# Strassen on four of eight blocks in the second MLP product, with a new way out of PSUM for its results

## The chip, the core and the metric

The kernel runs on one core of a Trainium2 chip, in one launch. The metric is the device time of a run in microseconds (us). Five engines matter: TensorE (PE in the profile, its weight loads PEld), VectorE (DVE), ScalarE (ACT), and SyncE (SP), which issues the weight transfers. GpSimd (POOL) has next to nothing to do.

## The reference

Two layers over 256 tokens of width 2048, all in float32. Each layer is a mixer and a dense MLP, each behind an RMS norm and added to the residual stream. The mixers (a short convolution beside differential attention in layer 0, forgetting attention in layer 1) are not touched by the change. The MLP is

```
def _sqrelu_mlp(h, w1, w2):
    return jnp.square(jax.nn.relu(h @ w1)) @ w2
...
        h = _rmsnorm(x, norm2_g[l])
        x = x + _sqrelu_mlp(h, mlp_w1[l], mlp_w2[l])
```

with `w1` of 2048 x 8192 and `w2` of 8192 x 2048, in both layers.

## The kernel before

**Precision.** A float32 product is made of three matmuls on split operands: each operand is a high part (a copy rounded to fp32r) and a low part (the rest), and `products` adds high x high, high x low and low x high into one PSUM bank (L635, L636, L637). The weights arrive as float32 in a tile `raw` (1 MB, 3 buffers). `split_w` makes `wh` on ScalarE (L146) and, from it, `wl` on VectorE (L147), 3 buffers each, so a split can start only when TensorE is through with the tile three back.

**The MLP.** `mlp` goes over 4 groups of 2048 hidden units. In a group, `hidden` makes 8 blocks of 256 hidden units by the first product (`gemm_t`, L564 and L568), and each block's result is squared, split and put away (`take`, `fill`). Then `gemm_pair` makes the second product twice: for output columns 0 to 1023 (n = 0) and 1024 to 2047 (n = 2). Here these two are called the first and the second product of a group, and their blocks 0 to 7. There are 16 products in all, 8 in each layer.

**Two kinds of block.** A block is 256 hidden units by 1024 output columns, for 256 tokens. `KINDS` says how each is made. Kind C is plain: 8 products into four banks, 24 matmuls. Kind S is Strassen's method: 7 products, 21 matmuls, into the banks P2, Q3, Q4 (shared with C blocks) and P1, Q5, P7, P6 (for S alone). For it VectorE first makes four sums of weights in a tile `T` (L652, L654, L655), and a second split is made, of `T` (`wb`), beside that of the weights (`wa`). P1, P2 and Q3 use `wa`, the first half of a block; Q5, P7, P6 and Q4 use `wb`, the second half.

```
    KINDS = "SCSCSCCC"
```

**Ends of a product.** When the last S block is done, its four own banks are added up in SBUF (tile `E`, L681 to L684) and added to the residual `xr` (L689): the early sums. The four shared banks are added to `xr` by four VectorE instructions that read PSUM (`final`, L695). `final` is put on the list `late`, which `flush` empties in the next product, behind the splits of its first block.

**Order.** The code is written as one stream, and the tile framework's scheduler then sets the order on each engine. It moves instructions past each other on an engine, single matmuls too, but each engine's queue then runs in that order. The order on VectorE is the same in the two products of all 8 groups.

Of the kernel before, what the change touches and what calls it, by code (L numbers as in the profile page):

```python
# [16 lines left out]
P = 128  # L17
D = 2048
# [8 lines left out]
def trunk_kernel(  # L27
# [54 lines left out]


    pending = []
    late = []

    def flush():

        while late:
            late.pop(0)()  # L90

    def step():

# [56 lines left out]
    def gemm(acts, w, c0, first=False):  # L150

        acc = []
        total = 4 * len(acts)
        i = 0
        for ai, a in enumerate(acts):
            raw = wraw.tile([P, 4, CW], F32, name="raw")
            src = w[a.row:a.row + CW, c0:c0 + CW].rearrange("(k p) n -> p k n", p=P)
            if first and ai == 0:
                for h in range(4):
                    nc.sync.dma_start(raw[:, h, :], src[:, h, :])  # L160
            else:
                nc.sync.dma_start(raw, src)
            wh, wl = split_w(raw, parts=4 if first and ai == 0 else 2 if first else 1)
            if i == 0:
                flush()
                acc += [accp.tile([P, CW], F32, name="acc") for _ in range(2)]
            until(lambda: a.left <= 0)
            if first and ai == 0:
                idle(6)
            for h in range(2):  # L170
                kk = (2 * h, 2 * h + 1)

                seq = [(t, k, p) for k in kk for p in (0, 2, 1) for t in range(2)]
# [65 lines left out]
    nlam = const.tile([P, 1], F32, name="nlam")  # L239
    bfb = const.tile([P, 16], F32, name="bfb")  # L240
    GP = 16 * 32 + 96
    gw = const.tile([P, KT, 16], F32, name="gw")
    gws = const.tile([P, GP], F32R, name="gws")

    def setup():
        rows = work.tile([P, 2 * P], F32, name="y")[:, :P]
        lv = work.tile([P, 12 * P], F32, name="ob", bufs=1)[:, :2 * P].rearrange("p (v d) -> p v d", v=4)
        nc.scalar.dma_start(rows[0:32], norm2_g.rearrange("l (k p) -> (l k) p", p=P))
        nc.scalar.dma_start(rows[32:56], hyb_conv_w[0].rearrange("w (k p) -> (w k) p", p=P))
        for c in range(0, P, 64):  # L250
            nc.scalar.dma_start(rows[56:57, c:c + 64], hyb_dq_g)
            nc.scalar.dma_start(rows[57:58, c:c + 64], hyb_dk_g)
        nc.scalar.dma_start(rows[58:59], hyb_subln_g)
        nc.scalar.dma_start(rows[59:60], fox_q_g)
        nc.scalar.dma_start(rows[60:61], fox_k_g)
        for i, v in enumerate((hyb_lq1, hyb_lk1, hyb_lq2, hyb_lk2)):
            nc.scalar.dma_start(lv[:, i, :], v.broadcast_to([P, 64]))
        nc.scalar.dma_start(bfb, fox_b_f.broadcast_to([P, 16]))
        nc.scalar.dma_start(gw, fox_w_in[0, :, 3 * D:3 * D + 16].rearrange("(k p) n -> p k n", p=P))


        nc.gpsimd.memset(mask, 0.0)
        for b in (0, 2):
            nc.gpsimd.affine_select(
                out=mask[:, b * P:(b + 1) * P], in_=mask[:, b * P:(b + 1) * P], pattern=[[-1, P]],
                compare_op=ALU.is_ge, fill=NEG, base=0, channel_multiplier=1)
        nc.gpsimd.memset(ones, 1.0)
        nc.gpsimd.affine_select(
            out=triu, in_=ones, pattern=[[1, P]], compare_op=ALU.is_ge, fill=0.0, base=0,
            channel_multiplier=-1)  # L270
        yield
# [153 lines left out]

    def forget_gates(nm):

        wv = gws[:, :KT * 32].rearrange("p (k n) -> p k n", n=32)
        nc.scalar.copy(gws[:, KT * 32:], ones[:, :96])
        nc.scalar.copy(wv[:, :, 0:16], gw)  # L430
# [115 lines left out]
    def gemm_t(acts, w, c0):  # L546
# [3 lines left out]
        for c in range(2):  # L550
            raw = wraw.tile([P, 8, 2 * P], F32, name="raw")
            r0 = c * 8 * P
            nc.sync.dma_start(raw, w[r0:r0 + 8 * P, c0:c0 + 2 * P].rearrange("(k p) n -> p k n", p=P))
            wh, wl = split_w(raw, (8, 2 * P))
            if c == 0:
                flush()
                acc += [accp.tile([P, CW], F32, name="acc") for _ in range(2)]
            for h in range(2):
                a = acts[2 * c + h]
                until(lambda: a.left <= 0)  # L560
                for f, k, p in TORDER:
                    fs = slice(f * P, (f + 1) * P)
                    if p == 0:
                        nc.tensor.matmul(  # L564
                            acc[f], wh[:, 4 * h + k, fs], a.both[:, k, :, :].rearrange("p s t -> p (s t)"),
                            start=c + h + k == 0, stop=False)
                    else:
                        nc.tensor.matmul(acc[f][:, 2 * P:], wl[:, 4 * h + k, fs], a.hi[:, k, :], start=False,  # L568
                                         stop=(c, h, k) == (1, 1, 3))
                step()  # L570
# [1 line left out]

    KINDS = "SCSCSCCC"

    class PairS:

# [27 lines left out]
    def hidden(nm, w, c0):  # L606

        pairs, half = [], None
        for i, kind in enumerate(KINDS):
# [2 lines left out]
                p = PairS()  # L612
            elif half is not None:
                p, half = PairC(half), None
            elif "C" in KINDS[i + 1:]:
                t = actp.tile([P, 4, 2, 2 * P], F32R, name="act")
                p, half = PairC(t[:, :2]), t[:, 2:]
            else:
# [17 lines left out]
        nc.tensor.matmul(acc, a[0], b[1], start=False, stop=False)  # L636
        nc.tensor.matmul(acc, a[1], b[0], start=False, stop=last)  # L637

    def gemm_pair(pairs, w, r0, n, r2, done):

        B = {}
        live = set()
        for i, (kind, p) in enumerate(zip(KINDS, pairs)):
# [12 lines left out]
                wa, wb = split_w(raw[:, 1:4]), split_w(T)  # L656
            else:
                wa = split_w(raw)
            if i == 0:
                flush()  # L660
                for nm in ("P2", "Q3", "Q4", "X"):
                    B[nm] = accp.tile([P, CW], F32, name="acc")
                for nm in ("P1", "Q5", "P7", "P6"):
# [11 lines left out]
            else:  # L675
                for k in range(2):
                    for bank, t, h in (("P2", 0, 1), ("Q3", 0, 0), ("X", 1, 0), ("Q4", 1, 1)):
                        mul(bank, p.part(k, t), wa, 2 * k + h, not more and k == 1)
            if i == KINDS.rindex("S") + 1:
                E = qkv.tile([P, 4, CW], F32, name="qk")  # L680
                nc.scalar.copy(E[:, 3], B["P1"])  # L681
                nc.vector.tensor_tensor(E[:, 2], B["P6"], E[:, 3], ALU.add)
                nc.vector.tensor_tensor(E[:, 1], B["P7"], E[:, 2], ALU.add)
                nc.vector.tensor_tensor(  # L684
                    E[:, 0:3:2], B["Q5"].unsqueeze(1).broadcast_to([P, 2, CW]), E[:, 1:3], ALU.subtract)
                for t in (1, 0):
                    x2 = xall[:, n:n + 2, t, :]
                    e = E[:, 2 - 2 * t:4 - 2 * t]
                    nc.vector.scalar_tensor_tensor(x2, e, r2[:, t:t + 1], x2, ALU.mult, ALU.add)  # L689
                done(0)  # L690
            step()

        def final():
            for bank, m, t in (("P2", n + 1, 0), ("Q3", n, 0), ("X", n, 1), ("Q4", n + 1, 1)):
                nc.vector.scalar_tensor_tensor(  # L695
                    xr[m][:, t, :], B[bank], r2[:, t:t + 1], xr[m][:, t, :], ALU.mult, ALU.add)
                done(1, m, t)
        late.append(final)

    def mlp(nm, l, nxt):  # L700
        ov = out[0].rearrange("(t p) d -> p t d", p=P)
        r2 = None
        for g in range(4):
# [5 lines left out]
            for n in (0, 2):  # L709
                def done(stage, m=None, t=None, n=n, g=g):  # L710
# [7 lines left out]
                        pending.extend([nxt.chunk(0), nxt.chunk(1)])  # L718
                    elif n == 2 and (m, t) == (n + 1, 1):
                        pending.extend([nxt.chunk(2), nxt.chunk(3)])  # L720
                gemm_pair(pairs, mlp_w2[l], g * D, n, r2, done)
        if nxt is None:
            flush()

    def load_x(n):
        if n > 0:
# [69 lines left out]
```

## Time and profile before

| | |
|---|---|
| three runs | median 2175.74 us (2175.13 to 2176.91) |
| profiled execution | 2178.49 us |
| its span, first to last instruction | 2176.8 us |
| TensorE busy | 2166.2 us (100%) |
| VectorE busy | 1547.4 us (71%) |
| ScalarE busy | 1052.7 us (48%) |
| granted TensorE clock | 1.0 of full |

The sums of the prediction are made against the profiled execution, 2178.49 us, which is 2.75 us above the median. Busy shares are means over the whole span: the stages differ.

### The profile page before, as it was taken

How to read it: one execution, taken by the hardware profiler on the slowest of the kernel's cores; microseconds unless marked ns; L12 is line 12 of the kernel's file. 1: busy time of each engine (PE TensorE's matmuls, PEld its weight loads, DVE VectorE, ACT ScalarE, POOL GpSimd, SP SyncE). 2: the span in 40 equal slices, each digit the busy share in tenths (PEclk: the TensorE clock that was granted, in tenths of full speed). 3: DMA queues.
4: the chain of work that ended last, by engine and by line, in shares of the span. 5: the costliest groups of instructions: out<-in, count | busy, mean ns of one | idle time of the engine just before them, and what ended most of it. 6: DMA issues, size and time to landing. Idle time of an engine off the chain costs nothing. (4 is left out here: it accounts for less than half of the span.)

```text
span 2176.8 us, 26071 instructions
## 1 busy us (share of the span) xinstructions
PE 2166.2 (100%) x10738; PEld 1818.3 (84%) x10738; DVE 1547.4 (71%) x1574; ACT 1052.7 (48%) x1101; POOL 19.1 (1%) x17
## 2 busy tenths in 40 slices
PE   9999999999999999999999999999999999999999
PEld 7887888888888888888888888888888888888887
DVE  5666655778769768767855565567787697687687
ACT  6455443544444444445554454445444444444453
POOL 0000000000000000000000000000000000000000
PEclk9999999999999999999999999999999999999999
DMA  8544556555665665665645555555566656656654
GB/s 272 180 159 158 187 177 200 178 167 198 220 193 170 220 193 182 211 189 190 210 163 194 187 183 173 185 166 176 168 207 216 193 174 216 190 191 207 186 192 151
DMA packets 245273, 412.08 MB, mean 189 GB/s; under 512 B 9399, under 2 KB 144802, under 8 KB 245154
## 3 DMA queue, kind: packets, MB, share of 16 engines
q1 hardware_dynamic: 237296, 405.84, 57.6%
q10 hardware_dynamic: 7858, 4.58, 0.7%
q8 instruction: 84, 1.38, 0.3%
q14 instruction: 35, 0.29, 0.0%
HBM read 408.28 MB, written 2.11 MB: 189 GB/s over the span
## 5 line engine op out<-in xcount | busy, mean ns | idle before, releaser
L147 DVE TENSOR_TENSOR wl<-raw,wh 128x2048 fp32r<-128x2048 f32 (+3 forms) x390 | 855.7, 2196 | 476.8 <-ACT wh L146 476.3
L146 ACT CAST wh<-raw 128x2048 fp32r<-128x2048 f32 (+3 forms) x390 | 713.6, 1832 | 654.3 <-PE acc L179 232.0
L564 PE MATMUL acc<-act,wh 128*128 128x512 f32 x2048 | 643.8, 396 | 0.0
L179 PE MATMUL acc<-wh,act 128*128 128x512 f32 x2048 | 565.0, 397 | 0.1
L568 PEld LDWEIGHTS acc<-act,wl 128*128 128x128 f32 x2048 | 384.7, 188 | 90.7
L179 PEld LDWEIGHTS acc<-wh,act 128*128 128x128 f32 x2048 | 376.5, 188 | 75.3 <-issue 2.0
L568 PE MATMUL acc<-act,wl 128*128 128x256 f32 x2048 | 402.4, 278 | 0.0
L179 PE MATMUL acc<-wl,act 128*128 128x512 f32 x1024 | 318.8, 391 | 0.3 <-DVE wl L147 0.3
L564 PEld LDWEIGHTS acc<-act,wh 128*128 128x128 f32 x2048 | 312.3, 189 | 0.8
L636 PE MATMUL acc<-wl,act 128*128 128x512 f32 x656 | 256.1, 390 | 2.1 <-DVE wl L147 1.9
L637 PE MATMUL acc<-wh,act 128*128 128x512 f32 x656 | 255.3, 389 | 0.0
L635 PE MATMUL acc<-wh,act 128*128 128x512 f32 x656 | 251.5, 389 | 0.0
L179 PEld LDWEIGHTS acc<-wl,act 128*128 128x128 f32 x1024 | 192.1, 188 | 42.8 <-issue 0.7
L636 PEld LDWEIGHTS acc<-wl,act 128*128 128x128 f32 x656 | 123.1, 188 | 30.7 <-DVE wl L147 5.2
L635 PEld LDWEIGHTS acc<-wh,act 128*128 128x128 f32 x656 | 123.1, 188 | 25.7
L637 PEld LDWEIGHTS acc<-wh,act 128*128 128x128 f32 x656 | 123.2, 188 | 25.3
L146 ACT CAST wh<-qk 128x2048 fp32r<-128x2048 f32 x48 | 91.8, 1913 | 92.9 <-DVE qk L655 68.7
L147 DVE TENSOR_TENSOR wl<-qk,wh 128x2048 fp32r<-128x2048 f32 x48 | 109.9, 2290 | 22.2 <-ACT wh L146 21.6
L626 ACT COPY qk<-acc 128x256 f32<-128x256 f32 x128 | 47.1, 368 | 132.4 <-PE acc L568 132.4
L635 PE MATMUL tp<-wh,act 128*128 128x512 f32 x192 | 74.7, 389 | 0.0
L636 PE MATMUL tp<-wl,act 128*128 128x512 f32 x192 | 74.7, 389 | 0.0
L637 PE MATMUL tp<-wh,act 128*128 128x512 f32 x192 | 74.7, 389 | 0.0
(173 smaller groups left out, 1434.4 us busy)
## 6 DMA issues: line engine op xcount, KB each, us to landing
raw<-in_mlp_w_dram SPq DMA_DIRECT2D x256, 1024.0 KB, 5.5
raw<-in_fox_w_in_dram SPq DMA_DIRECT2D x48, 1024.0 KB, 5.2
raw<-in_hyb_w_in_dram SPq DMA_DIRECT2D x47, 1024.0 KB, 5.2
raw<-in_hyb_w_out_dram SPq DMA_DIRECT2D x16, 1024.0 KB, 5.2
raw<-in_fox_w_out_dram SPq DMA_DIRECT2D x16, 1024.0 KB, 5.1
ob<-fcd ACTq DMA_DIRECT2D x4, 512.0 KB, 4.5
xr<-in_x_dram SPq DMA_DIRECT2D x3, 512.0 KB, 7.4
raw<-in_hyb_w_in_dram SPq DMA_DIRECT2D x4, 256.0 KB, 4.5
```

Of the source, the lines that this page charges most:

```text
L146: nc.scalar.copy(wh[:, s], src[:, s])
L147: nc.vector.tensor_tensor(wl[:, s], src[:, s], wh[:, s].bitcast(F32), ALU.subtract)
L179: nc.tensor.matmul(acc[t], x, (wl if p == 1 else wh)[:, k, :], start=st, stop=sp)
L564: nc.tensor.matmul(acc[f], wh[:, 4 * h + k, fs], a.both[:, k, :, :].rearrange("p s t -> p (s t)"), start=c + h + k == 0, stop=False)
L568: nc.tensor.matmul(acc[f][:, 2 * P:], wl[:, 4 * h + k, fs], a.hi[:, k, :], start=False, stop=(c, h, k) == (1, 1, 3))
L626: nc.scalar.copy(fj, acc[j][:, 2 * P:])
L635: nc.tensor.matmul(acc, a[0], b[0], start=not started, stop=False)
L636: nc.tensor.matmul(acc, a[0], b[1], start=False, stop=False)
L637: nc.tensor.matmul(acc, a[1], b[0], start=False, stop=last)
```

## The change

1. `KINDS` becomes `SCSSCSCC`: four S blocks and four C blocks, in places 0, 2, 3, 5 and 1, 4, 6, 7.
2. The early sums are made at the head of block 7 (two after the last S block, before the block's matmuls) and no longer behind those of the block after the last S.
3. The four shared banks are taken out of PSUM by ScalarE (four `activation` copies with the scale `r2`, into a tile `F`), and VectorE adds `F` to `xr` in one instruction over 128 x 2048. That addition is put on a second list, `later`, emptied behind the splits of block 1 of what follows. Only the last product of the program ends as before (`tail`).
4. In `hidden`, C blocks 6 and 7 keep their operands in the two `v` buffers. The forget gate's weights are loaded and split in tiles of the pools `work` and `act`, no longer in tiles of their own.

```
-    late = []
-
-    def flush():
-
-        while late:
-            late.pop(0)()
+    late, later = [], []
+
+    def flush(held):
+
+        while held:
+            held.pop(0)()
...
-            if i == 0:
-                flush()
+            if i > 0:
+                flush(later)
+            else:
+                flush(late)
...
-    KINDS = "SCSCSCCC"
+    KINDS = "SCSSCSCC"
...
-            elif "C" in KINDS[i + 1:]:
+            elif i < 3:
...
-    def gemm_pair(pairs, w, r0, n, r2, done):
+    def gemm_pair(pairs, w, r0, n, r2, done, tail):
...
-            if i == KINDS.rindex("S") + 1:
+            if i == 1:
+                flush(later)
+            if i == KINDS.rindex("S") + 2:
                 E = qkv.tile([P, 4, CW], F32, name="qk")
                 nc.scalar.copy(E[:, 3], B["P1"])
                 nc.vector.tensor_tensor(E[:, 2], B["P6"], E[:, 3], ALU.add)
...
         def final():
-            for bank, m, t in (("P2", n + 1, 0), ("Q3", n, 0), ("X", n, 1), ("Q4", n + 1, 1)):
-                nc.vector.scalar_tensor_tensor(
-                    xr[m][:, t, :], B[bank], r2[:, t:t + 1], xr[m][:, t, :], ALU.mult, ALU.add)
-                done(1, m, t)
...
+            F = qkv.tile([P, 4, CW], F32, name="qk")
+            for bank, j in (("P2", 2), ("Q3", 0), ("X", 1), ("Q4", 3)):
+                nc.scalar.activation(F[:, j], B[bank], AF.Copy, scale=r2[:, j % 2:j % 2 + 1])
+
+            def add():
+                x4 = xall[:, n:n + 2].rearrange("p m t n -> p (m t) n")
+                nc.vector.tensor_tensor(x4, x4, F, ALU.add)
+                for j in range(4):
+                    done(1, n + j // 2, j % 2)
+            later.append(add)
         late.append(final)
```

**First place: VectorE in the middle of a first product (layer 0, group 1).** In the rows of before, `wl_5057` is the low part of block 2's sums, `qk_5113` holds the sums of block 4, and `wl_5084` is the low part of block 3, a C block:

```order
L147 TENSOR_TENSOR wl_5057<-qk_5048,wh_5056 128x2048
L600 TENSOR_TENSOR v_4964<-qk_4979,v_4964 128x2x256
L652 TENSOR_TENSOR qk_5113<-raw_5111 128x1024
L654 TENSOR_TENSOR qk_5113<-qk_5113,raw_5111 128x512
L655 TENSOR_TENSOR qk_5113<-qk_5113,raw_5111 128x512
L147 TENSOR_TENSOR wl_5084<-raw_5081,wh_5083 128x2048
L147 TENSOR_TENSOR wl_5118<-raw_5111,wh_5117 128x1536
```

In the changed kernel block 3 is an S block: `qk_5102` holds its sums, `wl_5107` and `wl_5111` are its two low parts, `qk_5167` are the sums of block 5 and `wl_5138` is the low part of block 4:

```order
L147 TENSOR_TENSOR wl_5076<-qk_5067,wh_5075 128x2048
L606 TENSOR_TENSOR v_4983<-qk_4998,v_4983 128x2x256
L658 TENSOR_TENSOR qk_5102<-raw_5100 128x1024
L660 TENSOR_TENSOR qk_5102<-qk_5102,raw_5100 128x512
L661 TENSOR_TENSOR qk_5102<-qk_5102,raw_5100 128x512
L147 TENSOR_TENSOR wl_5107<-raw_5100,wh_5106 128x1536
L658 TENSOR_TENSOR qk_5167<-raw_5165 128x1024
L147 TENSOR_TENSOR wl_5111<-qk_5102,wh_5110 128x2048
L147 TENSOR_TENSOR wl_5138<-raw_5135,wh_5137 128x2048
```

The sums made here are those of block 3 in place of block 4's, and one more instruction of 1024 and one of 2048 stand between block 3's first low part and block 4's.

**Second place: VectorE at the start of a second product (same group).** Before, `wl_5250` and `wl_5254` are the low parts of block 0, `qk_5322` the sums of block 2, and `wl_5293` is the low part of block 1:

```order
L147 TENSOR_TENSOR wl_5250<-raw_5243,wh_5249 128x1536
L655 TENSOR_TENSOR qk_5245<-qk_5245,raw_5243 128x512
L652 TENSOR_TENSOR qk_5322<-raw_5320 128x1024
L654 TENSOR_TENSOR qk_5322<-qk_5322,raw_5320 128x512
L695 SCALAR_TENSOR_TENSOR xr_87<-acc_4987,r2_3711,xr_87 128x512
L147 TENSOR_TENSOR wl_5254<-qk_5245,wh_5253 128x2048
L695 SCALAR_TENSOR_TENSOR xr_87<-acc_4988,r2_3711,xr_87 128x512
L695 SCALAR_TENSOR_TENSOR xr_87<-acc_4990,r2_3711,xr_87 128x512
L695 SCALAR_TENSOR_TENSOR xr_87<-acc_4989,r2_3711,xr_87 128x512
L147 TENSOR_TENSOR wl_5293<-raw_5290,wh_5292 128x2048
```

In the changed kernel `wl_5274` and `wl_5278` are the low parts of block 0, `qk_5281` is `F`, `wl_5318` is the low part of block 1, `qk_5348` and `qk_5383` are the sums of blocks 2 and 3, and `wl_5357` is the second low part of block 2:

```order
L661 TENSOR_TENSOR qk_5269<-qk_5269,raw_5267 128x512
L147 TENSOR_TENSOR wl_5274<-raw_5267,wh_5273 128x1536
L147 TENSOR_TENSOR wl_5278<-qk_5269,wh_5277 128x2048
L714 TENSOR_TENSOR xr_87<-xr_87,qk_5281 128x2048
L147 TENSOR_TENSOR wl_5318<-raw_5315,wh_5317 128x2048
L658 TENSOR_TENSOR qk_5348<-raw_5346 128x1024
L147 TENSOR_TENSOR wl_5353<-raw_5346,wh_5352 128x1536
L660 TENSOR_TENSOR qk_5348<-qk_5348,raw_5346 128x512
L658 TENSOR_TENSOR qk_5383<-raw_5381 128x1024
L661 TENSOR_TENSOR qk_5348<-qk_5348,raw_5346 128x512
L660 TENSOR_TENSOR qk_5383<-qk_5383,raw_5381 128x512
L661 TENSOR_TENSOR qk_5383<-qk_5383,raw_5381 128x512
```

The wide addition now stands between the low parts of blocks 0 and 1, where three of the four PSUM reads stood, and the sums of two blocks follow ahead of `wl_5357`, which is the next row.

**The same place on ScalarE.** Before, the high parts of blocks 0, 1 and 2 of the second product follow one another (`wh_5249` and `wh_5253`, `wh_5292`, `wh_5326` and `wh_5330`):

```order
L146 CAST wh_5249<-raw_5243 128x1536
L146 CAST wh_5253<-qk_5245 128x2048
L146 CAST wh_5292<-raw_5290 128x2048
L146 CAST wh_5326<-raw_5320 128x1536
L146 CAST wh_5330<-qk_5322 128x2048
```

Now the four copies out of PSUM stand among them:

```order
L146 CAST wh_5273<-raw_5267 128x1536
L710 ACTIVATE qk_5281<-acc_5006,r2_3712 128x512
L146 CAST wh_5277<-qk_5269 128x2048
L710 ACTIVATE qk_5281<-acc_5007,r2_3712 128x512
L710 ACTIVATE qk_5281<-acc_5009,r2_3712 128x512
L710 ACTIVATE qk_5281<-acc_5008,r2_3712 128x512
L146 CAST wh_5317<-raw_5315 128x2048
```

The high part of block 0's sums (`wh_5277`) moved behind the first of the copies, and that of block 1 behind all four.

## Rows read from the trace of the kernel before

**Rows 1.** The page's first part: engine, busy us (share of the span), instructions.
```profile
PE 2166.2 (100%) x10738; PEld 1818.3 (84%) x10738; DVE 1547.4 (71%) x1574; ACT 1052.7 (48%) x1101; POOL 19.1 (1%) x17
```
**Rows 2.** Stretches of group 1, layer 0: hidden blocks, first product, second product.
```profile
core 0: us, PE busy (x) PEld busy (x) DVE busy (x) ACT busy (x) POOL busy (x), PEclk, DMA share, GB/s
567.65:656.82 89.17, 89.17 (x514) 77.81 (x513) 60.40 (x61) 40.02 (x39) 0.00 (x0) 1.00 0.61 189
656.82:698.65 41.83, 41.78 (x186) 34.28 (x185) 37.03 (x31) 20.90 (x14) 0.00 (x0) 1.00 0.58 193
698.65:740.16 41.51, 41.51 (x185) 34.35 (x183) 35.72 (x26) 20.49 (x12) 0.00 (x0) 1.00 0.64 211
```
**Rows 3.** L636's own view: its engine's idle time (us, times), by what ended it.
```profile
  DVE wl L147: 7.1, 11
```
**Rows 4.** Timeline, first product: start us, us, engine, line [idle before <- releaser].
```profile
671.79 0.39 PE L635 MATMUL acc<-wh,act 128*128 128x512 f32 x1
...
672.22 0.19 PEld L636 LDWEIGHTS acc<-wl,act 128*128 128x128 f32 x1 [0.47 <-DVE wl L147]
672.22 0.50 PE L636 MATMUL acc<-wl,act 128*128 128x512 f32 x1
```
**Rows 5.** Timeline of VectorE in the first product, from the second low part of block 2.
```profile
664.05 2.29 DVE L147 TENSOR_TENSOR wl<-qk,wh 128x2048 fp32r<-128x2048 f32 x1 [0.42 <-ACT wh L146]
666.26 0.68 DVE L600 TENSOR_TENSOR v<-qk,v 128x512 fp32r<-128x512 f32 x1
667.28 1.23 DVE L652 TENSOR_TENSOR qk<-raw 128x1024 f32<-128x1024 f32 x1 [0.34 <-DMA raw<-in_mlp_w_dram]
668.54 0.69 DVE L654 TENSOR_TENSOR qk<-qk,raw 128x512 f32<-128x512 f32 x1
669.27 0.69 DVE L655 TENSOR_TENSOR qk<-qk,raw 128x512 f32<-128x512 f32 x1
669.88 3.95 DVE L147 TENSOR_TENSOR wl<-raw,wh 128x2048 fp32r<-128x2048 f32 x2
```
**Rows 6.** Timeline of VectorE, end of the first and start of the second product.
```profile
679.71 2.29 DVE L147 TENSOR_TENSOR wl<-raw,wh 128x2048 fp32r<-128x2048 f32 x1 [3.44 <-ACT wh L146]
681.92 0.69 DVE L682 TENSOR_TENSOR qk<-tp,qk 128x512 f32<-128x512 f32 x1
682.52 2.28 DVE L147 TENSOR_TENSOR wl<-raw,wh 128x2048 fp32r<-128x2048 f32 x1
...
688.66 1.21 DVE L652 TENSOR_TENSOR qk<-raw 128x1024 f32<-128x1024 f32 x1
689.79 2.47 DVE L689 SCALAR_TENSOR_TENSOR xr<-qk,r,xr 128x1024 f32<-128x1024 f32 x2
692.18 0.68 DVE L654 TENSOR_TENSOR qk<-qk,raw 128x512 f32<-128x512 f32 x1
692.78 1.75 DVE L147 TENSOR_TENSOR wl<-raw,wh 128x1536 fp32r<-128x1536 f32 x1
694.45 0.68 DVE L655 TENSOR_TENSOR qk<-qk,raw 128x512 f32<-128x512 f32 x1
...
701.75 2.28 DVE L147 TENSOR_TENSOR wl<-raw,wh 128x2048 fp32r<-128x2048 f32 x1
```
**Rows 7.** Timeline of ScalarE in the same stretch.
```profile
677.76 1.91 ACT L146 CAST wh<-raw 128x2048 fp32r<-128x2048 f32 x1 [3.82 <-PE acc L637]
...
687.97 1.49 ACT L146 CAST wh<-raw 128x1536 fp32r<-128x1536 f32 x1 [3.52 <-PE acc L637]
```
**Rows 8.** Timeline of TensorE at block 1 of the second product.
```profile
703.41 1.07 PE L635 MATMUL acc<-wh,act 128*128 128x512 f32 x4
704.31 0.39 PE L635 MATMUL tp<-wh,act 128*128 128x512 f32 x1
704.54 0.39 PE L636 MATMUL acc<-wl,act 128*128 128x512 f32 x1
```
**Rows 9.** Groups by line: busy us, mean ns of one, idle before.
```profile
L695 DVE SCALAR_TENSOR_TENSOR xr<-acc,r,xr 128x512 f32<-128x512 f32 x64 | 44.3, 743 | 5.5 <-PE acc L637 5.5
L229 ACT ACTIVATE qk<-acc,rstd 128x512 f32<-128x512 f32 x32 | 20.7, 683 | 0.9 <-PE acc L179 0.9
```
**Rows 10.** Timeline where layer 0's MLP ends (1086.4) and layer 1's first projection begins.
```profile
1084.79 0.87 DVE L136 SCALAR_TENSOR_TENSOR act<-tp,g,act 128x256 fp32r<-128x256 f32 x2
...
1086.38 0.60 PE L198 MATMUL tp<-ident,xr 128*128 128x128 f32 x4
...
1088.38 0.83 ACT L135 ACTIVATE act<-tp,g 128x256 fp32r<-128x256 f32 x2
```

More of the change, by code (lines that the diff above doesn't have):

```diff
@@ L241, in trunk_kernel @@
     GP = 16 * 32 + 96
-    gw = const.tile([P, KT, 16], F32, name="gw")
-    gws = const.tile([P, GP], F32R, name="gws")
     def setup():
@@ L258, in setup @@
         nc.scalar.dma_start(bfb, fox_b_f.broadcast_to([P, 16]))
-        nc.scalar.dma_start(gw, fox_w_in[0, :, 3 * D:3 * D + 16].rearrange("(k p) n -> p k n", p=P))
         nc.gpsimd.memset(mask, 0.0)
@@ L426, in forget_gates @@
     def forget_gates(nm):
+        gt = actp.tile([P, 16 * P], F32R, name="act")
+        gws = gt[:, :GP]
+        gw = work.tile([P, 2 * P], F32, name="y").rearrange("p (k n) -> p k n", n=16)
+        nc.scalar.dma_start(gw, fox_w_in[0, :, 3 * D:3 * D + 16].rearrange("(k p) n -> p k n", p=P))
+        yield
         wv = gws[:, :KT * 32].rearrange("p (k n) -> p k n", n=32)
@@ L554, in gemm_t @@
             wh, wl = split_w(raw, (8, 2 * P))
-            if c == 0:
-                flush()
+            if c > 0:
+                flush(later)
+            else:
+                flush(late)
                 acc += [accp.tile([P, CW], F32, name="acc") for _ in range(2)]
@@ L658, in gemm_pair @@
                 wa = split_w(raw)
+            if i == 1:
+                flush(later)
+            if i == KINDS.rindex("S") + 2:
+                E = qkv.tile([P, 4, CW], F32, name="qk")
+                nc.scalar.copy(E[:, 3], B["P1"])
+                nc.vector.tensor_tensor(E[:, 2], B["P6"], E[:, 3], ALU.add)
+                nc.vector.tensor_tensor(E[:, 1], B["P7"], E[:, 2], ALU.add)
+                nc.vector.tensor_tensor(
+                    E[:, 0:3:2], B["Q5"].unsqueeze(1).broadcast_to([P, 2, CW]), E[:, 1:3], ALU.subtract)
+                for t in (1, 0):
+                    x2 = xall[:, n:n + 2, t, :]
+                    e = E[:, 2 - 2 * t:4 - 2 * t]
+                    nc.vector.scalar_tensor_tensor(x2, e, r2[:, t:t + 1], x2, ALU.mult, ALU.add)
+                done(0)
             if i == 0:
-                flush()
+                flush(late)
                 for nm in ("P2", "Q3", "Q4", "X"):
@@ L678, in gemm_pair @@
                         mul(bank, p.part(k, t), wa, 2 * k + h, not more and k == 1)
-            if i == KINDS.rindex("S") + 1:
[L680 to L690, printed above, removed]
             step()
         def final():
-            for bank, m, t in (("P2", n + 1, 0), ("Q3", n, 0), ("X", n, 1), ("Q4", n + 1, 1)):
-                nc.vector.scalar_tensor_tensor(
-                    xr[m][:, t, :], B[bank], r2[:, t:t + 1], xr[m][:, t, :], ALU.mult, ALU.add)
-                done(1, m, t)
+            if tail:
+                for bank, m, t in (("P2", n + 1, 0), ("Q3", n, 0), ("X", n, 1), ("Q4", n + 1, 1)):
+                    nc.vector.scalar_tensor_tensor(
+                        xr[m][:, t, :], B[bank], r2[:, t:t + 1], xr[m][:, t, :], ALU.mult, ALU.add)
+                    done(1, m, t)
+                return
+            F = qkv.tile([P, 4, CW], F32, name="qk")
[7 more added lines that the diff above has]
+            later.append(add)
         late.append(final)
@@ L720, in done @@
                         pending.extend([nxt.chunk(2), nxt.chunk(3)])
-                gemm_pair(pairs, mlp_w2[l], g * D, n, r2, done)
+                gemm_pair(pairs, mlp_w2[l], g * D, n, r2, done, nxt is None and g == 3 and n == 2)
         if nxt is None:
-            flush()
+            flush(late)
     def load_x(n):
```

## The prediction

> **What bounds the kernel now.** I read the page's busy times first: TensorE is busy for the whole span, VectorE for 71%, ScalarE for 48% [rows 1]. Then the stretches of one group: in the hidden blocks VectorE has room (60.4 of 89.2 us), but in the two products it is busy for 37.0 of 41.8 and 35.7 of 41.5 us [rows 2]. That is where the change adds VectorE work, so those two lines matter and not the 71%. The second product's stretch holds its 183 matmuls (the row counts two of its neighbours), 41.51 / 183 = 0.2268 us each; I write m for it. An S block is 21 m = 4.76 us, a C block 24 m = 5.44 us. Last, who makes TensorE wait there: the second of the three matmuls of a sum (L636) for the low part of the weights, 11 times, 7.1 us of idle engine in all [rows 3]. In the instance shown the weight load was idle for 0.47 us, but the matmul came 0.43 us after the one before it, so TensorE lost 0.43 - 0.23 = 0.20 us [rows 4]. By that ratio the 7.1 us cost 3.0 us. So TensorE is the bound, and VectorE stands close behind it in the products.
>
> **What is removed from TensorE.** A product has 4 x 21 + 4 x 24 = 180 matmuls, three fewer. 16 products, 48 matmuls, 48 m = **-10.9 us**.
>
> **What VectorE gets.** One more S block in a product: sums of 1.21 + 0.69 + 0.69, a second low part of 2.29, and a first one of 1.75 in place of 2.29, together +4.35 us [rows 5, 6]. The first product then needs 37.0 + 4.35 = 41.4 us of VectorE against 180 m = 40.8 us of TensorE. In the second product the four PSUM reads go (4 x 0.743 us, [rows 9]) and the wide addition comes. Before has no such instruction; the nearest is L147, also two float32 operands in SBUF over 128 x 2048, 2.29 us, and I take that. The upper end is two L689 of 1024, 2.47 us; the lower end is 2.2, L147's distance to the next start. The second product needs 35.7 + 4.35 - 2.97 + 2.29 = 39.4 us. Both together: 80.8 us of VectorE in 81.6 of TensorE. With only three weight tiles ahead, an in-order queue can't be 99% busy without being late, so I follow it through one group. All eight have this order.
>
> The change rests on the copies to SBUF sparing VectorE, and the trace prices that at 2.97 - 2.29 = 0.68 us a product. The Trainium skill (VectorE: DVE Perf Modes, The perf-mode tier table) speaks against more: a float32 addition of two tensors makes one result a cycle, from SBUF as from PSUM, and for 2048 elements it gives 2293 ns. By that figure the sum below stays as it is; if its doubled rate for one source applied (1227 ns), each group would wait 1.07 us less, 8.5 us in all.
>
> **First product.** Clock zero is its first matmul (656.82 before). The VectorE rows up to the hidden result of block 7 (L600) are the same as before; it started at 666.26, so at 9.44. Distances between starts, from the rows: 0.61 after a 512 when the next is independent, 0.73 when it is not; 1.13 and 1.26 after a 1024; 1.67 after 1536; 2.21 after 2048 [rows 5, 6]. Block 3's sums start at 10.05 and their last at 12.04; its first low part at 12.65, block 5's first sum at 14.32, block 3's second low part from 15.45 to 17.74. TensorE wants that after 66 + 9 matmuls and two high-part matmuls that the order has pulled ahead: 77 m = 17.46. **It waits 0.3 us.** The waits of before go: there the sums of block 4 stood in this place and waited for their transfer [rows 5], which made block 3's low part late; block 3's tile was asked for a whole block earlier. So -3.0 us for the old waits, all told.
>
> **Second product.** Clock zero now is the first matmul of block 5 of the first product; the second product begins 69 m = 15.65 later. Block 6's high part may start when block 4 is done; before, block 4 began at 656.82 + 90 m + 0.3 = 677.5, the high part of block 5 waited for that and started 0.2 later, took 1.91, and the low part followed at 679.71 [rows 6, 7]. So block 6's low part starts at 2.15. Nine rows from there without a wait (2.21, 0.60, 2.21, 0.60, 1.13, 1.13, 0.60 and 2.39 for the two that were L689, [rows 6]) bring VectorE to the last sum of block 0 at 13.0, ready at 13.7, and to its first low part, done at 15.4. Its second low part needs ScalarE's high part, and ahead of that stands the copy of P2. That bank's last matmul is over at 15.65 - 10 m + 0.39 = 13.8; the copy costs 0.68 (L229, also from PSUM with a scale, [rows 9]; the next starts 0.62 later), so the high part runs from 14.4 to 16.3. The low part runs to 18.65, the wide addition starts at 18.55, and block 1's low part runs from 20.75 to 23.05. TensorE does 13 matmuls to 18.6, waits 0.15, is in block 1 at 20.6, does four high-part matmuls and one of block 2 ahead (as it did before, [rows 8]), and **from 21.7 waits 1.45 us** for block 1's low part.
>
> It then has 20 + 8 matmuls, to 29.5. VectorE meanwhile: a sum, a low part of 1536, five sums of blocks 2 and 3, to 29.4; block 2's sums were ready at 28.2, so their high part is there at 30.1 and the low part at 32.4. TensorE does four high-part matmuls from 30.15, three of block 3 and sits at 32.5: **1.5 us lost**. 26 matmuls later, at 38.4, block 4 does five, to 39.55, and its low part (queue: 1.67 + 2.21 + 1.13 + 2.29 from 32.3) is there at 39.7: **0.15**. From there VectorE keeps ahead. Lost in a second product: 0.15 + 1.45 + 1.5 + 0.15 = 3.25 us; in a group 3.55; in eight, **+28.4 us**.
>
> **The other edits.** At the end of layer 0's MLP the transposes for the next norm stood among the last blocks' matmuls and their splits ahead of `final`. With later sums they all follow the last matmul, and the first low part (L136, 0.48) stands behind the wide addition, which waits for the four copies: 0.85 + 2.21 + 0.48 = 3.55 after the last matmul. Eight transposes (0.9) and the first high part (0.47 behind the copies, at 1.3) leave TensorE idle for 0.4 and, after two matmuls, from 1.75 for 1.85: **+2.3 us**, once [rows 10]. At nothing: the extra `fill` of an S block in `hidden` (1.5 us of VectorE a group), hidden in the 29 us that VectorE has free there; without that room it would be 12 us. Also at nothing: the gate weights, asked for a whole MLP before use, and the tiles of blocks 6 and 7, whose buffers were last read a group before.
>
> **The sum.** -10.9 - 3.0 + 28.4 + 2.3 = +16.8; 2178.5 + 16.8 = 2195.3 profiled, and 2.75 less for the median: **2192.5 us**, slower by 0.8%. Its own range: the order of the rows is fixed, but each clock above may be off by half a us, and waits may run from 2.3 to 4.8 us a group; the dearer wide addition (+0.2, 1.6 us in all) lies within that. 2183 to 2203.
>
> **The rivals.** (a) *TensorE stays fed; faster.* For it: the busiest engine at 100%, and VectorE would come to about 75% of the span. Then -10.9 and -3.0 come in, the end of layer 0 costs 2.3, and the time is 2164. It needs VectorE ahead at block 1 of the second product, 1.5 us earlier than I find it; the break-even is 11.6 / 8 = 1.45 us lost a group. Against it: 80.8 of 81.6. The Trainium skill (Perfetto Trace Analysis, Identifying the Most-Contended Engine) names this rule, to judge by the engine of highest occupancy; the trace agrees over the span and not in the products. 17%.
> (b) *VectorE loses more:* ScalarE's copies make the high parts of blocks 1 and 2 late as well, and the first product enters late, because block 5's sums are split up between low parts. A further 1.5 us a group gives 2204 or more. For it: ScalarE's order puts block 1's high part behind four copies. Against: it is done at 20.1, before VectorE asks. 13%.
> (c) *The waits are half of mine,* 1.3 to 2.3 us a group: between nothing and +0.3%, 2174 to 2183; the half below 2180 is within 0.2%. 14%.
> (d) *My forecast,* 56%.
>
> **Chances and range.** A difference under 0.2% (4.4 us) is about what a measurement of this kernel can't tell from no change. Faster: 0.17 from (a). Same: 0.08, half of (c) and the upper edge of (a). Slower: the rest, 0.75. The range of 8 in 10 runs from 2172, within (c) and above (a), to 2207.
>
> **What would show it.** In the new profile: 10690 matmuls; TensorE's waits for L147's low part some 29 us in total, most on the second products, block 1 and block 2, none over 2 us; VectorE near 97% busy in the products' stretches; the wide addition at 2.3 us; a gap of about 2 us after layer 0's last product. If the stretches of a second product take 41 us and not 44, the queue walk is wrong, and the likeliest place is block 0's second high part on ScalarE.

## The result, and the profile after

The changed kernel takes 2197.24 us (median of 4 runs, 2195.94 to 2197.40) against 2176.28 us before on the same chip (2175.13 to 2176.91): by all runs compared 1.0093 times as long, 95% interval 1.0080 to 1.0105 (the two medians alone give 1.0096). It is slower. The profiled execution took 2195.94 us with a span of 2194.1 us at full granted clock, 17.3 us more than the span of before.

The page's first part, and the group of the second matmul of a sum for the shared banks (busy us, mean ns | idle before it, and what ended it):

```profile
PE 2169.3 (99%) x10690; PEld 1804.2 (82%) x10690; DVE 1612.1 (73%) x1617; ACT 1112.8 (51%) x1177; POOL 15.4 (1%) x17
...
L642 PE MATMUL acc<-wl,act 128*128 128x512 f32 x448 | 176.5, 394 | 9.3 <-DVE wl L147 9.3
```

48 matmuls are gone, and the page still shows TensorE busy for 3 us more. Part of each wait reads as busy: rows of matmuls are 0.39 us long but start 0.23 apart, so the first 0.16 us of a wait are covered, and a matmul that has waited reads longer (0.50 us below) than one that hasn't. So the time lost is read from the starts of the matmuls. The stretches of group 1 in layer 0 (hidden blocks, first product, second product; columns as in [rows 2]) show where the time went:

```profile
568.21:657.37 89.16, 89.16 (x513) 77.80 (x512) 63.02 (x63) 41.23 (x41) 0.00 (x0) 1.00 0.62 191
657.37:698.40 41.03, 41.03 (x183) 33.71 (x181) 37.47 (x31) 22.31 (x16) 0.00 (x0) 1.00 0.51 179
698.40:742.66 44.26, 42.44 (x181) 33.23 (x180) 40.65 (x28) 25.79 (x20) 0.00 (x0) 1.00 0.66 212
```

180 matmuls at 0.2268 us are 40.8 us. The first product loses 0.2 us over that, the second 3.46, and the hidden blocks are as long as before. All eight groups read alike: first products 40.98 to 41.03, second 44.27 to 44.34.

VectorE at the start of this second product (698.40), from block 0's first low part (L147, 1536) to block 2's second; L714 is the wide addition:

```profile
696.42 1.75 DVE L147 TENSOR_TENSOR wl<-raw,wh 128x1536 fp32r<-128x1536 f32 x1
699.13 2.29 DVE L147 TENSOR_TENSOR wl<-qk,wh 128x2048 fp32r<-128x2048 f32 x1 [0.96 <-ACT wh L146]
701.34 2.28 DVE L714 TENSOR_TENSOR xr<-xr,qk 128x2048 f32<-128x2048 f32 x1
703.54 2.29 DVE L147 TENSOR_TENSOR wl<-raw,wh 128x2048 fp32r<-128x2048 f32 x1
...
713.02 2.29 DVE L147 TENSOR_TENSOR wl<-qk,wh 128x2048 fp32r<-128x2048 f32 x1 [0.73 <-ACT wh L146]
```

ScalarE in the same place: the copies out of PSUM are L710, the high parts L146.

```profile
696.61 0.69 ACT L710 ACTIVATE qk<-acc,r 128x512 f32<-128x512 f32 x1 [7.40 <-PE acc L643]
697.19 1.91 ACT L146 CAST wh<-qk 128x2048 fp32r<-128x2048 f32 x1
698.99 1.85 ACT L710 ACTIVATE qk<-acc,r 128x512 f32<-128x512 f32 x3
700.71 3.31 ACT L146 CAST wh<-raw 128x2048 fp32r<-128x2048 f32 x2
...
711.08 1.91 ACT L146 CAST wh<-qk 128x2048 fp32r<-128x2048 f32 x1 [7.07 <-DVE qk L661]
```

And TensorE where it waits, at block 1 (705.88), and at blocks 2 and 3 (from 713.04):

```profile
705.88 0.50 PE L642 MATMUL acc<-wl,act 128*128 128x512 f32 x1 [1.18 <-DVE wl L147]
706.22 0.40 PE L643 MATMUL acc<-wh,act 128*128 128x512 f32 x1
...
713.04 0.98 PE L641 MATMUL tp<-wh,act 128*128 128x512 f32 x3 [0.48 <-ACT wh L146]
...
714.42 0.50 PE L641 MATMUL tp<-wh,act 128*128 128x512 f32 x1 [0.16 <-ACT wh L146]
...
715.37 0.50 PE L642 MATMUL tp<-wl,act 128*128 128x512 f32 x1
```

The addition's end (703.54 by the next start) is the start of block 1's low part, and that one's end (705.83) is the start of TensorE. ScalarE is named at 713.04, but its own row (711.08) had waited 7.07 us for VectorE's sums (L661): the late engine is VectorE both times.

At the end of layer 0 the last product ends at 1091.6 and eight transposes follow; then TensorE waits for the first high and the first low part of the next norm, the latter behind the wide addition:

```profile
1091.63 1.03 PE L200 MATMUL tp<-ident,xr 128*128 128x128 f32 x8
1092.93 0.73 PE L181 MATMUL acc<-wh,act 128*128 128x512 f32 x2 [0.27 <-ACT act L135]
1095.29 0.74 PE L181 MATMUL acc<-wh,act 128*128 128x512 f32 x2 [1.62 <-DVE act L136]
...
1092.55 2.29 DVE L714 TENSOR_TENSOR xr<-xr,qk 128x2048 f32<-128x2048 f32 x1
1094.76 1.65 DVE L136 SCALAR_TENSOR_TENSOR act<-tp,g,act 128x256 fp32r<-128x256 f32 x4
```

### The profile page after: what moved, and what is told of

Read it like the earlier page. It is cut to its first block, busy times and chain, and to the rows that moved or that the text cites. A ratio compares the mean times of both kernels' runs of the same rounds, so it can differ in the third digit from the quotient of the medians.

```text
span 2194.1 us, 26099 instructions
## 1 busy us (share of the span) xinstructions
PE 2169.3 (99%) x10690; PEld 1804.2 (82%) x10690; DVE 1612.1 (73%) x1617; ACT 1112.8 (51%) x1177; POOL 15.4 (1%) x17
## 4 chain that ended last, share of the span: by engine, by line
PE 92%; DVE 5%; ACT 2%; issue 1%; DMA 0%; SPq 0%; ACTq 0%
PE acc L181 32%; PE acc L570 22%; PE acc L574 11%; PE acc L642 6%; PE acc L643 6%; PE acc L641 6%; DVE wl L147 3%; PE tp L642 2%; PE tp L643 2%; PE tp L641 2%; ACT wh L146 1%; DVE qk L658 1%; DVE xr L714 1%; PE tp L200 0%; PE tp L318 0%
## 5 line engine op out<-in xcount | busy, mean ns | idle before, releaser
L147 DVE TENSOR_TENSOR wl<-raw,wh 128x2048 fp32r<-128x2048 f32 (+3 forms) x390 | 848.0, 2177 | 412.8 <-ACT wh L146 412.4
L146 ACT CAST wh<-raw 128x2048 fp32r<-128x2048 f32 (+3 forms) x390 | 704.9, 1815 | 530.4 <-PE acc L181 238.8
L181 PE MATMUL acc<-wh,act 128*128 128x512 f32 x2048 | 565.9, 397 | 2.5 <-DVE act L136 1.8
L181 PEld LDWEIGHTS acc<-wh,act 128*128 128x128 f32 x2048 | 375.6, 188 | 79.3 <-DVE act L136 3.4
L181 PE MATMUL acc<-wl,act 128*128 128x512 f32 x1024 | 318.7, 391 | 0.0
L181 PEld LDWEIGHTS acc<-wl,act 128*128 128x128 f32 x1024 | 192.1, 188 | 42.8 <-issue 0.7
L146 ACT CAST wh<-qk 128x2048 fp32r<-128x2048 f32 x64 | 122.3, 1911 | 149.5 <-DVE qk L661 128.1
L147 DVE TENSOR_TENSOR wl<-qk,wh 128x2048 fp32r<-128x2048 f32 x64 | 146.6, 2290 | 61.4 <-ACT wh L146 60.9
L642 PE MATMUL acc<-wl,act 128*128 128x512 f32 x448 | 176.5, 394 | 9.3 <-DVE wl L147 9.3
L643 PE MATMUL acc<-wh,act 128*128 128x512 f32 x448 | 174.8, 390 | 0.0
L641 PE MATMUL acc<-wh,act 128*128 128x512 f32 x448 | 166.2, 391 | 0.0
L642 PEld LDWEIGHTS acc<-wl,act 128*128 128x128 f32 x448 | 84.1, 188 | 32.1 <-DVE wl L147 15.0
L642 PE MATMUL tp<-wl,act 128*128 128x512 f32 x256 | 102.5, 401 | 0.0
L643 PE MATMUL tp<-wh,act 128*128 128x512 f32 x256 | 100.0, 391 | 0.0
L641 PEld LDWEIGHTS acc<-wh,act 128*128 128x128 f32 x448 | 84.1, 188 | 19.0 <-ACT qk L710 1.9
L643 PE MATMUL acc<-wh,v 128*128 128x512 f32 x256 | 99.6, 389 | 0.0
L642 PE MATMUL acc<-wl,v 128*128 128x512 f32 x256 | 99.6, 389 | 0.0
```

Of the source, the lines that this page charges most:

```text
L146: nc.scalar.copy(wh[:, s], src[:, s])
L147: nc.vector.tensor_tensor(wl[:, s], src[:, s], wh[:, s].bitcast(F32), ALU.subtract)
L641: nc.tensor.matmul(acc, a[0], b[0], start=not started, stop=False)
```

## The experiments

The theory is the prediction's: in the two products VectorE is an in-order queue with hardly any slack, and what it does there decides, instruction by instruction, how late a low part is. The rivals blame one edit (the exit through ScalarE, the place of the wide addition) or one product alone. Stage lengths below are read from TensorE's starts in each trace, as those above.

**The four S blocks without the other edits** (`e1_kinds_only`), from before:

```
-    KINDS = "SCSCSCCC"
+    KINDS = "SCSSCSCC"
...
-            elif "C" in KINDS[i + 1:]:
+            elif i < 3:
```

> Only the fourth S block is changed; the banks leave PSUM and the sums are made as before. Queue theory (TensorE waits for a VectorE queue that is late by its order and its sum, and the way out over ScalarE adds to it): block 0's second low part of a second product is not held up by a PSUM copy, the four PSUM reads (4 x 0.66) stand where the wide addition stood, block 1's low part is ready 0.65 us earlier than in the changed kernel, a second product takes 43.6 us instead of 44.3, and the late end of layer 0 shrinks: 2188 to 2192 us, 5 to 9 less than the changed kernel. Rival (only the amount of VectorE work counts): 0.68 us more VectorE work a product on a full queue, 2200 to 2204 us.

Measured: 2197.49 us (2197.20 to 2197.66), ratio 1.0095 (1.0078 to 1.0112), span 2195.9. The second products came as the queue walk says, 43.65 us, but the total missed both ranges: the hidden blocks after them became 1.6 us longer, which nobody had expected. First before, at the end of that product, then this kernel:

```profile
566.57 2.72 DVE L695 SCALAR_TENSOR_TENSOR xr<-acc,r,xr 128x512 f32<-128x512 f32 x4
```
```profile
565.92 2.29 DVE L147 TENSOR_TENSOR wl<-raw,wh 128x2048 fp32r<-128x2048 f32 x1
568.12 2.72 DVE L695 SCALAR_TENSOR_TENSOR xr<-acc,r,xr 128x512 f32<-128x512 f32 x4
...
569.01 0.70 PE L564 MATMUL acc<-act,wh 128*128 128x512 f32 x2 [1.38 <-DVE xr L695]
```

Before, the product ended at 567.65 and the four reads had begun 1.1 us ahead of that; here it ends at 567.47, VectorE is late and the reads begin 0.65 us behind it, and the first hidden matmul waits for a bank. So the exit through ScalarE frees the banks in time (1.6 us in each of six places), and costs 0.65 us in each second product and 2.6 more at the end of layer 0: between the two kernels 1.8 us of span. It is not what makes the change slow.

**The other edits without the fourth S block** (`e2_exit_only`), from after:

```
-    KINDS = "SCSSCSCC"
+    KINDS = "SCSCSCCC"
...
-            elif i < 3:
+            elif "C" in KINDS[i + 1:]:
```

> Three S blocks as before, with the new way out (four ScalarE copies, wide addition, sums later). Queue theory: TensorE's work is that of before; the wide addition stands ahead of block 1's low part and the second half of block 2 comes 0.5 to 1.4 us late in each second product, and the end of layer 0 costs 2 to 3 us: 2181 to 2190 us. Rival (amount of VectorE work): 0.68 us less on VectorE a product, so no new waits, and only the end of layer 0 costs: 2175 to 2179 us.

Measured: 2183.01 us (2181.90 to 2184.52), ratio 1.0029 (1.0018 to 1.0040). First products 41.75 us (0.25 gained each), second 41.95 (0.45 lost), end of layer 0 1.8 us longer. The queue theory holds, the rival is out.

**The wide addition one place later** (`e3_add_behind_block1`), from after; it is issued behind block 1's low part:

```
...
             if i == 1:
-                flush(later)
+                with tc.issue_after(last["lo"]):
+                    flush(later)
```

> The changed kernel with the wide addition forced behind block 1's low part on VectorE. Queue theory: the wait at block 1 shrinks from 1.3 us to about 0.3, but block 2's second low part comes no earlier, so the wait moves there and a second product still takes 44.0 to 44.4 us: 2195 to 2198 us, no change. Rival (the place of the wide addition is the cause): the 1.3 us at block 1 are gained in every group, 2186 us or less.

Measured: 2192.48 us (2191.53 to 2193.98), ratio 1.0073 (1.0058 to 1.0088). Its VectorE:

```profile
701.21 1.23 DVE L659 TENSOR_TENSOR qk<-raw 128x1024 f32<-128x1024 f32 x1
702.43 2.29 DVE L148 TENSOR_TENSOR wl<-raw,wh 128x2048 fp32r<-128x2048 f32 x1
704.63 2.28 DVE L716 TENSOR_TENSOR xr<-xr,qk 128x2048 f32<-128x2048 f32 x1
...
712.30 2.29 DVE L148 TENSOR_TENSOR wl<-qk,wh 128x2048 fp32r<-128x2048 f32 x1
```

The addition did change places with block 1's low part, but the scheduler also put block 2's first sum (L659, 1.23 us) ahead of that low part. TensorE's wait there fell from 1.34 to 0.42 us and not to nothing. The second low part of block 2 stands behind the addition in both kernels; it starts 14.1 us into the product in place of 14.6, and TensorE, through with block 1 0.9 us sooner, waits longer for it and for block 3: 1.57 us in place of 1.13. Second products 43.8, 0.5 gained each. Both numbers missed, the queue's by 2.5 us and the rival's by 6.5: moved by one place, the addition gives block 1 0.9 us, and half of that is lost again behind it.

**Hardly any wide addition** (`e4_no_add`), from after. It leaves out the addition of 504 of the 512 columns of each bank:

```
-                nc.vector.tensor_tensor(x4, x4, F, ALU.add)
+                nc.vector.tensor_tensor(x4[:, :, :8], x4[:, :, :8], F[:, :, :8], ALU.add)
```

> The changed kernel with the wide addition cut to 8 of 512 columns of each bank, so 2.0 us of VectorE work per product are left out (the other columns do not get these results). Queue theory: every later low part up to block 4 comes 2.0 us earlier, a second product takes 42.2 us, and the end of layer 0 is 2 us shorter: 2177 to 2181 us. Rival (ScalarE's high parts hold TensorE, as the releaser named at block 2 says): only the 1.3 us at block 1 can be gained, and half of that comes back at block 2: 2186 to 2192 us.

Measured: 2174.26 us, ratio 0.9988 (0.9978 to 0.9998). The two products of group 1:

```profile
654.97:695.95 40.98, 40.98 (x182) 33.72 (x181) 37.47 (x31) 22.30 (x16) 0.00 (x0) 1.00 0.53 180
695.95:737.72 41.77, 41.46 (x182) 33.48 (x181) 38.85 (x28) 26.04 (x20) 0.00 (x0) 1.00 0.70 225
```

And VectorE at the start of the second:

```profile
696.68 2.29 DVE L147 TENSOR_TENSOR wl<-qk,wh 128x2048 fp32r<-128x2048 f32 x1 [0.96 <-ACT wh L146]
698.89 0.18 DVE L714 TENSOR_TENSOR xr<-xr,qk 128x32 f32<-128x32 f32 x1
699.01 1.23 DVE L658 TENSOR_TENSOR qk<-raw 128x1024 f32<-128x1024 f32 x1
700.23 2.29 DVE L147 TENSOR_TENSOR wl<-raw,wh 128x2048 fp32r<-128x2048 f32 x1
...
707.90 2.28 DVE L147 TENSOR_TENSOR wl<-qk,wh 128x2048 fp32r<-128x2048 f32 x1
```

An addition of 32 elements takes 0.18 us, so the next row comes 2.1 us earlier, and the second product is 2.5 us shorter. The next row is not the same one: the scheduler put block 2's first sum there, so block 1's low part gains only 0.9 us and TensorE still waits 0.47 us for it. The waits at blocks 2 and 3 are gone, ScalarE's among them, though nothing of ScalarE was changed. It came out 2.7 us below the expected range: three of the four waits of a second product went entirely, and with each the 0.11 us that it had cost TensorE beyond itself (last section), 2.6 us over eight products.

**The fourth S block in one product only** (`g1_first_only`, `g2_second_only`), from the first experiment's kernel. Here is the first; in the second the two strings change places. Block 3 is then done plainly from the S tile, so the last S block is block 5 and not 4 as before.

```
-        for i, (kind, p) in enumerate(zip(KINDS, pairs)):
+        kinds = "SCSCCSCC" if n else KINDS
+        for i, (kind, p) in enumerate(zip(kinds, pairs)):
...
-                        mul(bank, p.part(k, t), wa, 2 * k + h, not more and k == 1)
+                        mul(bank, p.plain(k, t), wa, 2 * k + h, not more and k == 1)
```

> The kernel with the four S blocks and the old exit, but only the first product uses the four; the second works with three (blocks 0, 2 and 5; block 3 plainly). 24 matmuls fewer than before. What the two theories differ in is where the second product's loss is made: carried over by VectorE from the first product, or made by the second product's own fourth S block. Carried over: first products 41.0 us as in the kernel after (8 us gained over all eight), second products 42.3 in place of 41.5, with the wait at blocks 0 and 1 still there and that at blocks 2 and 3 gone, 2175 to 2178. Made by the second product itself: second products 41.5 as before, 2168 to 2170. Neither expects a wait at the start of the hidden blocks.

Measured: 2192.04 us (2191.52 to 2192.89), ratio 1.0071 (1.0056 to 1.0086): outside both ranges. First products 41.0 us, but second ones 43.3, and 1.2 us lost at each start of the hidden blocks. TensorE in the second product of group 1:

```profile
705.74 0.50 PE L639 MATMUL acc<-wl,act 128*128 128x512 f32 x1 [0.23 <-DVE wl L147]
713.70 0.96 PE L638 MATMUL acc<-wh,act 128*128 128x512 f32 x3 [0.41 <-ACT wh L146]
```

> The mirror image: the first product works with three S blocks (0, 2 and 5), the second with four, old exit. Carried over: VectorE enters the second product earlier, the wait at blocks 0 and 1 goes, that at blocks 2 and 3 becomes smaller, second products about 42.6 us and about 0.8 us of wait at the start of each hidden stage, 2188 to 2193. Made by the second product itself: second products 43.65 and 1.6 us at the hidden stage as with both, 2203 to 2206.

Measured: 2204.02 us (2202.21 to 2205.27), ratio 1.0128 (1.0111 to 1.0145). First products 42.3 to 43.0 us, second 42.6 to 43.1, and 1.6 us lost at each start of the hidden blocks. The total lies in the range of "made by the second product itself", its parts do not: that range needed second products of 43.65.

Read by place the two agree. The waits at blocks 0 and 1 of the second product stay when the first product has the four S blocks (about 1.0 us, as in the first experiment) and vanish when it has three: they are carried over. Those at blocks 2 and 3 stay when the second product has the four (1.4 us in the second of these kernels, 1.5 in the first experiment's) and are halved, to 0.68, when it has three: they are its own. These figures hold the 0.11 us behind each wait. Neither total can decide between the two. With the last S block at 5, as in the first experiment, the sums and reads of the exit come a block later than before, and the banks are late for the hidden blocks. And the first products of the second kernel, with 183 matmuls, lose 0.8 to 1.5 us, in group 1 nearly all at the low part of block 3; why that one is so late there is not shown.

**The wide addition where VectorE has room** (`h1_hold`), from after. `F` gets the `ob` buffer, widened to 16 P, so that it can live longer, and the addition goes behind the splits of block 6 of the next product:

```
-            if i == 1:
-                flush(later)
+            if i == 6:
+                with tc.issue_after(last["lo"]):
+                    flush(later)
...
-            F = qkv.tile([P, 4, CW], F32, name="qk")
+            F = work.tile([P, 16 * P], F32, name="ob", bufs=1).rearrange("p (j n) -> p j n", j=4)
```

> The changed kernel with F in a tile of its own (the attention's idle ob, widened to 8 KB) and the wide addition of a first product forced behind the low part of block 6 of the second. All the work is still done. Queue theory: 2.2 us leave the stretch before block 4, and the sums of block 2 no longer wait for F's buffer, so block 2's second low part comes before TensorE wants it; a second product takes 41.3 to 41.8 us instead of 44.3, the end of layer 0 stays: 2170 to 2176 us. Rival (the amount of VectorE work in the two products, 99%, is what counts, wherever it stands): the addition is still in the same product, the wait comes back at block 7 or in the hidden blocks, 2190 us or more.

Measured: 2180.52 us, ratio 1.0016 (1.0006 to 1.0026), 17 us below the changed kernel but 4.5 above the expected range. Of this kernel only the times are used; the next holds the same edit.

**The same, with the old exit at the end of each layer** (`h5_hold_end`):

```
-            if i == KINDS.rindex("S") + 2:
+            if i == KINDS.rindex("S") + (1 if tail else 2):
...
-                gemm_pair(pairs, mlp_w2[l], g * D, n, r2, done, nxt is None and g == 3 and n == 2)
+                gemm_pair(pairs, mlp_w2[l], g * D, n, r2, done, g == 3 and n == 2)
```

> As h1_hold, and the last product of each layer ends the old way (four PSUM reads on VectorE) with its sums one block earlier. Queue theory: 1.5 to 3 us less than h1_hold, all at the end of layer 0: 2168 to 2173 us. If the end of layer 0 cost nothing in the changed kernel, the same time as h1_hold.

Measured: 2179.11 us (2177.88 to 2180.61), ratio 1.0008 (0.9999 to 1.0018). Second products still lose 1.5 us, 6 us over the range in all: by the spacing of its matmuls 0.16, 0.45 and 0.45 at blocks 0, 1 and 3, and 0.11 behind each. The one at block 1 (0.29 is the idle engine alone):

```profile
702.81 0.50 PE L643 MATMUL acc<-wl,act 128*128 128x512 f32 x1 [0.29 <-DVE wl L148]
```

VectorE's rows show why the expectation failed:

```profile
695.80 1.22 DVE L659 TENSOR_TENSOR qk<-raw 128x1024 f32<-128x1024 f32 x1
696.94 2.29 DVE L148 TENSOR_TENSOR wl<-qk,wh 128x2048 fp32r<-128x2048 f32 x1
699.14 0.69 DVE L661 TENSOR_TENSOR qk<-qk,raw 128x512 f32<-128x512 f32 x1
699.86 0.69 DVE L662 TENSOR_TENSOR qk<-qk,raw 128x512 f32<-128x512 f32 x1
700.47 3.95 DVE L148 TENSOR_TENSOR wl<-raw,wh 128x2048 fp32r<-128x2048 f32 x2
...
711.47 1.23 DVE L659 TENSOR_TENSOR qk<-raw 128x1024 f32<-128x1024 f32 x1 [0.52 <-DMA raw<-in_mlp_w_dram]
712.61 2.29 DVE L148 TENSOR_TENSOR wl<-qk,wh 128x2048 fp32r<-128x2048 f32 x1
```

With the addition gone, the scheduler put the three sums of block 2 (L659, L661, L662) ahead of block 1's low part (700.47). And block 5's first sum (711.47) waits for its weights ahead of block 3's second low part, as in the first products of before [rows 5]. This edit also gives `F` a buffer of its own, which no run tries alone. The rows of the changed kernel speak against it as the cause: VectorE has no idle time to show from the wide addition (701.34) to block 3's last sum (711.61), so it waits for no buffer there.

**The second product begins with a C block** (`h3_cfirst`), from after:

```
-        for i, (kind, p) in enumerate(zip(KINDS, pairs)):
+        order = (1, 0, 2, 4, 3, 5, 6, 7) if n else range(8)
+        kinds = "".join(KINDS[b] for b in order)
+        for i, (b, kind) in enumerate(zip(order, kinds)):
+            p = pairs[b]
...
```

> The changed kernel with the second product's blocks in the order C S S C S S C C, so that it opens with a block that needs one low part and not two and four sums; F and the wide addition as in the change. Queue theory: the queue is 4.4 us less late at the opening, but the wide addition and F's buffer still stand ahead of the first S block's sums: a second product takes 42 to 43 us, 2178 to 2188 us. Rival (amount): no change, 2195 to 2199 us.

Measured: 2179.02 us (2177.95 to 2180.50), ratio 1.0010 (1.0000 to 1.0020), second products 42.1. A C block asks 2.29 us of VectorE for 5.44 us of TensorE; it lets the queue catch up just where it is carried over late. In group 1 no wait is left in the opening block; 1.0 us stays in the S block behind it.

**Both together** (`h4_cfirst_hold`): `h5_hold_end` with this order.

> As h5_hold_end with the order of h3_cfirst. Queue theory: a second product takes 40.9 to 41.3 us, nearly its 180 matmuls, 2164 to 2170 us, under h5_hold_end by 1 to 4 us. Rival (amount): like h5_hold_end or slower, since no VectorE work goes.

Measured: 2166.97 us (2165.96 to 2167.97), ratio 0.9952 (0.9937 to 0.9968): 30 us below the changed kernel and 10 below before, in the expected range. Page and the two products of group 1:

```profile
PE 2155.4 (100%) x10690; PEld 1807.3 (84%) x10690; DVE 1614.8 (75%) x1620; ACT 1118.2 (52%) x1173; POOL 17.0 (1%) x17
```
```profile
653.85:694.86 41.01, 41.01 (x183) 33.71 (x181) 37.70 (x31) 24.27 (x18) 0.00 (x0) 1.00 0.60 205
694.86:735.71 40.85, 40.85 (x181) 33.71 (x180) 38.94 (x27) 24.80 (x18) 0.00 (x0) 1.00 0.63 196
```

VectorE's total is nearly that of the changed kernel (1614.8 against 1612.1 us). What differs in the products is its order, and the second product loses 0.05 us in place of 3.46. VectorE's share of the two products has gone up, to 94% (37.70 + 38.94 of 81.86 us) from 92%, and TensorE doesn't wait: the share alone doesn't decide.

## Why the prediction was right

The mechanism and its places were right, and the sum against the trace came within 0.6 us: +16.8 forecast, +17.4 by the parts, +17.3 of span. That it came so close is in part luck: single terms are off by up to 1.7 us and cancel.

| term | forecast | measured |
|---|---|---|
| 48 matmuls | -10.9 | -10.9 (10690 left) |
| the old waits of first products | -3.0 | -4.1 (336.1 - 8 x 41.5) |
| first product, 8 x | +2.4 (0.3) | +1.6 (0.2) |
| second product, 8 x | +26.0 (3.25) | +27.7 (3.46) |
| end of layer 0 | +2.3 | +3.1 |

- **The queue walk.** From its clock zero (698.40 - 15.65 = 682.75) it put block 0's second high part at 697.15, the wide addition at 701.30, block 1's low part done at 705.80 and block 2's second low part done at 715.15; the rows have 697.19, 701.34, 705.83 and 715.31. By the spacing of the matmuls, restarts included (the 0.11 us that each wait costs beyond itself, last section), TensorE loses 0.20, 1.45, 1.46 and 0.11 us at blocks 0, 1, 2 with 3, and 4; forecast were 0.15, 1.45, 1.5 and 0.15. The other 0.24 lies in spacings too small to place. The walk did not know the restarts, 0.66 us in a second product. The waits without them are 0.09, 1.34, 1.13 and nothing, 2.56 us where 3.25 was forecast. Its own clocks give 1.35 at block 1 (21.7 to 23.05) and 1.4 at blocks 2 and 3, where it booked 1.45 and 1.5. So the places and the order of size were found, and the close agreement in size is luck.
- **The wide addition** takes 2.28 us, as L147 does. Here the Trainium skill (VectorE: DVE Perf Modes, The perf-mode tier table) agrees with the row: 2293 ns, no doubled rate.
- **The old waits** were under-sized. The scaling from one instance saw only the low part's view; whole first products of before lasted 41.5 to 43.2 us.
- **At nothing** was right for the extra `fill`: the hidden blocks last 89.16 us as before. Whether the gate weights cost anything was not tried by itself.
- **The end of layer 0** has the two waits of the walk (0.42 and 1.79 by spacing, forecast 0.4 and 1.85), but also 0.45 at 1105, where a later low part comes late, and restarts.
- **VectorE near 97% busy** in the products was wrong: 37.47 + 40.65 of 85.29 us, 92%. The forecast's own 80.8 us, over the 81.6 plus its 3.55 us of waits, are 95%. They hold whole durations, and consecutive rows overlap by 0.08 (701.34 to 703.54 is 2.20 for a row of 2.28); and more of the work than forecast lies in the hidden blocks (63.02 us where before has 60.40 [rows 2], with 1.5 expected). The walk went by starts and was not hurt. At 92% over two products the queue is still late where four S blocks, the exit and the addition meet.
- **The step that missed the median** is the last: "2.75 less for the median". The profiled execution of before was the slowest of its runs, that of after is the fastest, so the medians lie 21.0 us apart and the traces 17.3. What makes single runs of one kernel differ by 2 us is not shown here.
- **The rivals.** TensorE staying fed (a) was forecast at 2166.9 against the profiled execution; `h4_cfirst_hold`, where it does stay fed, has 2165.96. So the price of that case was near and its condition, VectorE ahead at block 1, was not met. Its terms cancel too: that kernel gains 4.1 us of old waits and not 3.0, still loses 0.2 us in each first product, and ends layer 0 the old way, for 0.7 us and not 2.3. ScalarE's copies do not make the high parts of blocks 1 and 2 late, as (b) has it: block 1's (700.71) is done before VectorE asks for it at 703.54, and the waits that name ScalarE vanish with 2.1 us of VectorE. What a copy does delay is block 0's second high part (697.19 behind 696.61), and VectorE idles 0.96 us for it (699.13), as the walk had it. The Trainium skill (Perfetto Trace Analysis, Identifying the Most-Contended Engine) would look to TensorE, whose weight loads are busy for 82% of the span; by `e4_no_add` 2.1 us of an engine at 73% are worth 2.5 us of time, because its limit lies in one stage.

## What to carry to other kernels

Where the second engine of a stage is nearly as busy as the first, follow its queue row by row from starts, over a whole group, since lateness made in one stage is paid in the next. Its share of the stage doesn't tell: here TensorE waited at 92% and didn't at 94%. Work that frees the busiest engine pays only if the second engine's work is also put where it has room: nearly the same instructions gave 2197 us in one order and 2167 in another. An edit that moves a late instruction by one place moves part of its wait, and the scheduler may put something else in the place that came free: read the new order before you judge the edit.

## What was not expected of the hardware

A matmul behind a wait is followed 0.34 us later by the next (705.88 to 706.22), not 0.23 later: each wait costs TensorE 0.11 us beyond itself. A second product of the changed kernel has four such places behind the waits shown, and two more (701.81 and 722.91) where only the weight load ahead had been idle: 0.66 of its 3.46 us.
